# Attention in a two-layer decoder trunk: scaling and transposing the probabilities one unit further behind the exponentials

## The chip, the cores and the metric

The kernel runs on one core of one Trainium2 chip. The metric is the device time of one execution in microseconds (us). One execution was also profiled. A core has five engines that run their own instruction streams and wait for each other by semaphores: PE (TensorE, matrix products; its weight loads are shown apart as PEld), DVE (VectorE), ACT (ScalarE), POOL (GpSimd) and SP (SyncE, which here only issues DMAs).

## The reference

Two layers over 1024 tokens of width 1024, in fp32. Layer 0 projects the normalized input to six parts, runs a gated linear recurrence (mixer A) and a sliding-window attention (mixer B) on them, gates both and projects them back. Layer 1 is a gated MLP with spatial mixing over chunks of 128 tokens. The change lies in mixer B; what it computes for a block of 128 queries and 256 keys is this:

```python
sc = jnp.einsum("bqkgd,bskd->bkgqs", qblk, kblk).astype(jnp.float32) * scale + bias
sc = jnp.where(mask, sc, -jnp.inf)
m = jnp.maximum(jnp.max(sc, axis=-1, keepdims=True), sink)
p = jnp.exp(sc - m)
denom = jnp.sum(p, axis=-1, keepdims=True) + jnp.exp(sink - m)
out = jnp.einsum("bkgqs,bskd->bqkgd", (p / denom).astype(vblk.dtype), vblk)
```

Before it q and k are RMS-normalized; after it the result is multiplied by SiLU of its gate path. Mixer A is a causal convolution of width 4, two sigmoid gates by block-diagonal products, and a scan over the tokens:

```python
xa = causal_depthwise_conv(za, conv_w[j], conv_b[j])
ya = rg_lru(xa, gate_a_w[j], gate_a_b[j], gate_x_w[j], gate_x_b[j], lru_lambda[j])
```

## The kernel before

All large products are done as three fp32r products of split operands (high*high, high*low, low*high; `mm3`, lines 145 to 147), so a weight tile comes in two parts: ACT makes `wh` (line 133) and DVE makes `wl` (line 134) from the raw tile that SP fetched (line 125). `load_weights` does this some tiles ahead.

Attention is cut into 32 units: four groups c of four heads, times eight blocks b of 128 queries; unit u is c = u // 8, b = u % 8. A unit has these steps, each a helper:

- `att_bias(u)` writes the bias, times the RMS of q, into the tile `e` (four heads by 256 keys; 128 keys in block 0): two heads by one POOL instruction (line 524), two by ACT (line 521).
- `att_s(u)`: PE makes the scores in two PSUM banks `ps` (lines 545 and 546); DVE adds them to `e` and takes the row maxima (line 549, four times), then makes `es`, sink minus maximum (line 557).
- `att_exp(u)`: ACT takes the exponentials of `es` (line 563) and of `e` head by head with their sums (line 565).
- `att_scale(u)`: DVE adds the two halves of the keys (line 573, not in block 0), makes the denominator and its reciprocal (lines 575 and 576) and multiplies (line 577). Adding the halves is allowed because the value product below works with differences of neighbouring value blocks.
- `att_pt(u)`: PE transposes the four heads into the bank `ppt` (line 585), ACT copies it to `ph` (588), DVE makes the rest `pl` (589), and POOL masks both into `mh` and `ml` (595, not in block 0).
- `att_pv(u)`: PE multiplies by the values, two to four products (605); ACT copies halves to `ot` (609, 610).
- `att_out(u)`: DVE adds (616, 617) and POOL multiplies into the gated result `yb` (619).

The loop over t runs these steps for different units side by side, and between them fillers for PE: in each pass 12 products of a projection of q or of `za`, and 12 of one of the gate paths (`gb`, later `ga`); every second pass also squares and copies q (`q_parts`, lines 491 to 495) and sums the squares on PE (`st`, line 503). In passes where t % 8 is 2, 3, 4 or 6 a weight tile is split. After the units two more passes empty the pipeline, each with 24 products of `ga` of channel block 1. Then mixer A begins (`mix_a_conv`, `mix_a_split`, `mix_a_gates`, ...), with `za` of channel block 2 as the first products on PE: 48 of them.

In the loop the order on PE, ACT, DVE and POOL is the order of the code. The order of PE stays that of the code to the end, and that of ACT and DVE too up to the convolution of channel block 1, although instructions of steps that come later in the code may be put between; from there a scheduler orders ACT, DVE and POOL. SP is left to the scheduler in the loop and behind it. `e` and `ot` each have two buffers before.

Of the kernel before, what the change touches and what calls it, by code (L numbers as in the profile page):

```python
# [11 lines left out]
F32 = mybir.dt.float32  # L12
# [6 lines left out]
P = 128  # L19
S = 1024  # L20
D = 1024
NT = S // P
# [18 lines left out]
def bc(ap, pos, n):  # L41

    dims = [list(d) for d in ap.ap]
    dims.insert(pos, [0, n])
    return bass.AP(tensor=ap.tensor, offset=ap.offset, ap=dims)


def flip(ap):

    dims = [list(d) for d in ap.ap]  # L50
    step, n = dims[-1]
    dims[-1] = [-step, n]
    return bass.AP(tensor=ap.tensor, offset=ap.offset + step * (n - 1), ap=dims)
# [8 lines left out]
def trunk_kernel(  # L62
# [10 lines left out]
    const = ctx.enter_context(tc.tile_pool(name="const", bufs=1))  # L73
# [6 lines left out]
    def bank(name):  # L80
        return ps.tile([P, 512], F32, tag="p", name=name)
# [373 lines left out]
    at = p1.enter_context(tc.tile_pool(name="at", bufs=2, reuse_waits="tile"))  # L455
# [4 lines left out]
    def bias_tile(hp):  # L460
        if hp not in bias_tiles:
            bt = at.tile([P, 2, 256], F32, tag="bias", name=f"bias{hp}")
            src = bass.AP(tensor=rdram.tensor, offset=rdram.offset + hp * 2 * 384,
                          ap=[[1, P], [384, 2], [1, 256]])
            nc.sync.dma_start(out=bt, in_=src)
            bias_tiles[hp] = bt
        return bias_tiles[hp]
# [31 lines left out]
    def q_stats(hc, p, sq):  # L499

        acc = bank(f"st{hc}_{p}")
        for b in range(4):
            nc.tensor.matmul(acc[:, 2 * b:2 * b + 2], lhsT=sq[:, b, :], rhs=pair_ones, start=True, stop=True)
        m = small.tile([P, 8], F32, tag="qm", name=f"qm{hc}_{p}", bufs=2)
        rs = small.tile([P, 8], F32, tag="qrs", name=f"qrs{hc}_{p}", bufs=5)
        rms = small.tile([P, 8], F32, tag="qrms", name=f"qrms{hc}_{p}", bufs=5)
        nc.vector.tensor_scalar(out=m, in0=acc[:, :8], scalar1=1.0 / HD, scalar2=EPS, op0=ALU.mult, op1=ALU.add)
        nc.gpsimd.tensor_tensor(out=rs, in0=m, in1=half_neg, op=ALU.pow)
        nc.gpsimd.tensor_tensor(out=rms, in0=m, in1=rs, op=ALU.mult)
        q_state[hc][1].append((rs, rms))  # L510

    def att_bias(u):

        c, b = units[u]
        k0 = 0 if b else P
        e = at.tile([P, 4, 256], F32, tag="e", name=f"e{u}")
        for hp in range(2):
            rms = q_state[2 * c + b // 4][1][hp][1]
            if hp:
                for j in range(2):  # L520
                    nc.scalar.mul(e[:, 2 + j, k0:256], bias_tile(2 * c + hp)[:, j, k0:256],
                                  rms[:, 2 * (b % 4) + j:2 * (b % 4) + j + 1])
                continue
            nc.gpsimd.tensor_tensor(out=e[:, 2 * hp:2 * hp + 2, k0:256], in0=bias_tile(2 * c + hp)[:, :, k0:256],
                                    in1=bc(rms[:, 2 * (b % 4):2 * (b % 4) + 2], 2, 256 - k0), op=ALU.mult)
        state[u]["e"], state[u]["k0"] = e, k0
# [41 lines left out]
    def att_scale(u):  # L568
        st = state[u]
        e = st["e"]  # L570
        p = st["p"] = e[:, :, 0:P] if units[u][1] else e[:, :, P:256]
        if units[u][1]:
            nc.vector.tensor_tensor(out=p, in0=p, in1=e[:, :, P:256], op=ALU.add)
        den = small.tile([P, 4], F32, tag="den", name=f"den{u}")
        nc.vector.tensor_tensor(out=den, in0=st["sums"], in1=st["es"], op=ALU.add)
        nc.vector.reciprocal(out=den, in_=den)
        nc.vector.tensor_tensor(out=p, in0=p, in1=bc(den, 2, P), op=ALU.mult)
# [3 lines left out]
    def att_pt(u):  # L581
        st = state[u]
        pt = bank(f"ppt{u}")
        for h in range(4):
            nc.tensor.transpose(pt[:, h * P:(h + 1) * P], st["p"][:, h, :], ident)
        ptv = pt.rearrange("p (j i s) -> p i j s", j=2, i=2)
        ph, pl = [at.tile([P, 2, 2, P], F32R, tag=f"p{r}", name=f"p{r}{u}", bufs=1) for r in "hl"]
        nc.scalar.copy(out=ph, in_=ptv)
        nc.vector.tensor_tensor(out=pl, in0=ptv, in1=ph.bitcast(F32), op=ALU.subtract)
        st["parts"] = [part.rearrange("p i j s -> p (i j s)") for part in (ph, pl)]  # L590
        st["before"] = []
        if units[u][1]:
            for r, part in zip("hl", st["parts"]):
                m = at.tile([P, 512], F32R, tag=f"m{r}", name=f"m{r}{u}", bufs=1)
                nc.gpsimd.affine_select(out=m, in_=part.bitcast(F32), pattern=[[0, 4], [1, P]], compare_op=ALU.is_ge,
                                        fill=0.0, base=-P, channel_multiplier=1)
                st["before"].append(m)

    def att_pv(u):
        c, b = units[u]  # L600
        st = state[u]
        acc = bank(f"pv{u}")
        terms = [(v_all, part) for part in st["parts"]] + [(v_more, part) for part in st["before"]]
        for n, (v, part) in enumerate(terms):
            nc.tensor.matmul(acc, lhsT=v[:, b, c // 2].rearrange("p r d -> p (r d)"), rhs=part, start=n == 0,
                             stop=n == len(terms) - 1)

        ot = at.tile([P, 256], F32, tag="ot", name=f"ot{u}")
        nc.scalar.copy(out=ot[0:HD, :], in_=acc[HD:P, 0:256])
        nc.scalar.copy(out=ot[HD:P, :], in_=acc[0:HD, 256:512])  # L610
        st["acc"], st["ot"] = acc, ot

    def att_out(u):
        c, b = units[u]
        acc, ot = state[u]["acc"], state[u]["ot"]
        nc.vector.tensor_tensor(out=ot[0:HD, :], in0=acc[0:HD, 0:256], in1=ot[0:HD, :], op=ALU.add)
        nc.vector.tensor_tensor(out=ot[HD:P, :], in0=acc[HD:P, 256:512], in1=ot[HD:P, :], op=ALU.add)
        y = yb[c][:, :, b * P:(b + 1) * P]
        nc.gpsimd.tensor_tensor(out=y, in0=flip(ot.rearrange("p (j s) -> p j s", j=2)), in1=y, op=ALU.mult)
        state[u] = None  # L620
# [4 lines left out]
    def mix_a_part(n, kind, half, khalf):  # L625

        if khalf == 0:
            mix_acc[n, kind, half] = bank(f"{kind}{n}_{half}")
        proj_stationary_w(mix_acc[n, kind, half], (kind, n), hh, hl, half * 512, khalf * 4, khalf * 4 + 4)

    def mix_a_product(n, kind):
        for half in range(2):
            for kh in range(2):
                mix_a_part(n, kind, half, kh)
# [9 lines left out]
    NU = len(units)  # L644
# [7 lines left out]
        q_step(0, j)  # L652
    q_stats(0, 0, sq)
    sq = q_parts(0, 1)
    for t in range(NU + 2):
        c, b = divmod(t, NT)
        new = t < NU
        hc, j = t // 4 + 1, t % 4
        q_done, evac = False, None
        if t >= 2:  # L660
            att_pt(t - 2)
        if new:
            if hc < 8:
                q_done = q_step(hc, j)
            else:
                mix_a_part(1, "za", j // 2, j % 2)
            if t == 0:
                q_stats(0, 1, sq)
        if 1 <= t <= NU:
            att_exp(t - 1)  # L670
        if new:
            att_bias(t)
        if new and c and b == 0:
            gb_silu(c)
        if new:
            evac = gb_step(c + 1, b // 4, (b // 2) % 2, b % 2) if c < 3 else mix_a_first(b)
        else:
            for kh in range(2):
                mix_a_part(1, "ga", t - NU, kh)
        if 1 <= t <= NU:  # L680
            att_scale(t - 1)
        if new and b in SPLIT_STEPS:
            load_weights(SPLIT_STEPS[b] + 4 * c)
        sq = q_parts(hc, j // 2) if q_done else None
        if evac:
            nc.scalar.copy(out=evac[0], in_=evac[1])
        if t >= 2:
            att_pv(t - 2)
        if q_done:
            q_stats(hc, j // 2, sq)  # L690
        if new:
            att_s(t)
        if t >= 2:
            att_out(t - 2)
    manual.__exit__(None, None, None)
    p1.close()

    def load_x1(src, tiles):

# [224 lines left out]

    manual = tc.manual_schedule(engines={ET.Activation, ET.DVE})
    manual.__enter__()
    mix_a_product(2, "za")
    conv = mix_a_conv(0)
    split = mix_a_split(0, conv)
    ys = [mix_a_silu(0)]  # L930
# [37 lines left out]
    p4 = ExitStack()  # L968
    late = {"po": p4.enter_context(tc.tile_pool(name="po", bufs=1, reuse_waits="tile"))}
    h1h, h1l = [[None] * 2 for _ in range(2)], [[None] * 2 for _ in range(2)]  # L970
    st_all = const.tile([P, NT, 8, 6], F32, name="st_all")

    def v_stats(t, g, src):
        for i in range(2):
# [463 lines left out]
```

## Time and profile before

| | |
|---|---|
| median of 3 runs | 1363.16 us (1361.72 to 1363.23) |
| the profiled execution | 1363.54 us, its span 1361.8 us |
| granted TensorE clock, mean | 0.997 |
| PE busy | 1322.3 us (97% of the span) |
| DVE busy | 1005.3 us (74%) |
| ACT busy | 692.1 us (51%) |
| POOL busy | 208.4 us (15%) |

The span runs from the first to the last instruction. The units of attention run from 86 us to 381 us of it. Matmuls are pipelined and their recorded ends are modelled, so a matmul's recorded duration is longer than the distance to the next. A number in square brackets behind a row is the idle time of that engine just before the row, and what ended it.

### The profile page before, as it was taken

The page shows a single profiled execution, that of the slowest core. Times are in us where ns is not written, and L with a number is a line of the kernel's source. Part 1 is how long each engine was busy: PE and PEld are TensorE (multiplying, and loading weights), DVE is VectorE, ACT ScalarE, POOL GpSimd, SP SyncE. Part 2 cuts the span into 40 slices and gives each one's busy share as a digit, 9 for nine tenths or more (in the row PEclk, how much of TensorE's full clock was granted, in tenths as well). Part 3 has the DMA queues.
Part 4 walks back from the last instruction along what each step waited for, and adds up shares of the span by engine and source line. Part 5 has one row for each costly group of instructions (what it writes and reads, how often), then busy time and mean ns, then how long its engine had stood idle before and what let it go on. Part 6 is the DMA issues. An engine that isn't in the chain of part 4 may idle for free.

```text
span 1361.8 us, 17820 instructions
## 1 busy us (share of the span) xinstructions
PE 1322.3 (97%) x6775; PEld 1122.1 (82%) x6775; DVE 1005.3 (74%) x1622; ACT 692.1 (51%) x1246; POOL 208.4 (15%) x212
## 2 busy tenths in 40 slices
PE   7999999999999999999999999999999999999998
PEld 6987777777788788888888999888888888888887
DVE  6568888888868888996987656566657656679874
ACT  6466767676568778433553323244433444333431
POOL 3344444443313223000000000000000000000000
PEclk9999999999999999999999999999999999999999
DMA  6111111111211203521423232413332233496131
GB/s 222 32 48 48 32 47 32 47 32 48 63 43 39 65 9 124 216 78 74 141 87 101 93 117 86 155 54 101 118 116 76 95 109 108 160 376 251 47 109 62
DMA packets 97170, 131.38 MB, mean 96 GB/s; under 512 B 4907, under 2 KB 68540, under 8 KB 95036
## 3 DMA queue, kind: packets, MB, share of 16 engines
q1 hardware_dynamic: 97084, 130.24, 28.6%
q8 instruction: 53, 0.87, 0.3%
q14 instruction: 33, 0.27, 0.1%
HBM read 105.03 MB, written 25.19 MB: 96 GB/s over the span
## 4 chain that ended last, share of the span: by engine, by line
PE 67%; DVE 19%; ACT 7%; DMA 3%; issue 3%; SPq 0%; DVEq 0%; ACTq 0%
PE m L145 6%; PE m L147 6%; PE m L146 6%; PE u L145 4%; PE u L147 4%; PE u L146 4%; PE g L145 3%; PE g L146 3%; PE g L147 3%; ACT e L565 3%; PE v L145 3%; PE v L146 3%; PE v L147 3%; DVE e L549 3%; PE s L1319 2%
## 5 line engine op out<-in xcount | busy, mean ns | idle before, releaser
L145 PE MATMUL m<-wh_w,wa 128*128 128x512 f32 x432 | 168.6, 390 | 1.8 <-DVE x L844 1.8
L147 PE MATMUL m<-wh_w,wa 128*128 128x512 f32 x432 | 168.1, 389 | 0.0
L146 PE MATMUL m<-wl_w,wa 128*128 128x512 f32 x432 | 168.1, 389 | 0.0
L145 PEld LDWEIGHTS m<-wh_w,wa 128*128 128x128 f32 x432 | 81.1, 188 | 19.3 <-ACT wa L709 2.6
L147 PEld LDWEIGHTS m<-wh_w,wa 128*128 128x128 f32 x432 | 81.1, 188 | 16.9
L146 PEld LDWEIGHTS m<-wl_w,wa 128*128 128x128 f32 x432 | 81.1, 188 | 16.7
L716 ACT CAST wh_w<-b 128x1024 fp32r<-128x1024 f32 x36 | 37.7, 1048 | 74.5 <-DVE b L811 54.2
L134 DVE TENSOR_TENSOR wl<-raw,wh 128x1024 fp32r<-128x1024 f32 x38 | 51.6, 1362 | 19.0 <-ACT wh L133 18.9
L549 DVE CUSTOM_DVE_ANT_0 e<-ps,e,sink_bc 128x256 f32<-128x256 f32 (+1 forms) x128 | 62.3, 524 | 3.7 <-PE ps L546 3.2
L565 ACT ACTIVATE e<-e,nm 128x256 f32<-128x256 f32 (+1 forms) x128 | 61.4, 481 | 0.0
L844 DVE TENSOR_TENSOR x<-m,x 128x512 f32<-128x512 f32 x56 | 36.6, 686 | 29.4 <-PE m L147 29.4
L145 PE MATMUL ga<-hh,wh 128*128 128x512 f32 x128 | 50.8, 397 | 2.2 <-DVE ya L888 2.2
L145 PE MATMUL pq<-hh,wh 128*128 128x512 f32 x128 | 52.4, 410 | 0.0
L1291 ACT ACTIVATE sg<-sg 128x512 f32<-128x512 f32 x24 | 15.2, 632 | 70.9 <-DVE sg L1290 70.9
L147 PE MATMUL pq<-hh,wl 128*128 128x512 f32 x128 | 50.3, 393 | 0.0
L146 PE MATMUL ga<-hl,wh 128*128 128x512 f32 x128 | 50.3, 393 | 0.0
L145 PE MATMUL gb<-hh,wh 128*128 128x512 f32 x128 | 50.2, 392 | 0.0
L145 PE MATMUL za<-hh,wh 128*128 128x512 f32 x128 | 50.2, 392 | 0.0
L146 PE MATMUL pq<-hl,wh 128*128 128x512 f32 x128 | 50.1, 392 | 0.0
L147 PE MATMUL ga<-hh,wl 128*128 128x512 f32 x128 | 50.1, 391 | 0.0
L717 DVE TENSOR_TENSOR wl_w<-b,wh_w 128x1024 fp32r<-128x1024 f32 x36 | 46.3, 1285 | 5.0 <-ACT wh_w L716 4.8
L147 PE MATMUL gb<-hh,wl 128*128 128x512 f32 x128 | 49.9, 390 | 0.0
(401 smaller groups left out, 4040.0 us busy)
## 6 DMA issues: line engine op xcount, KB each, us to landing
raw<-in_w_in_a_dram SPq DMA_DIRECT2D x34, 512.0 KB, 4.0
b<-in_w_out_a_dram SPq DMA_DIRECT2D x22, 512.0 KB, 3.4
b<-in_w_out_c_dram SPq DMA_DIRECT2D x22, 512.0 KB, 6.0
rawg<-in_w_in_c_dram SPq DMA_DIRECT2D x16, 512.0 KB, 3.5
rawu<-in_w_in_c_dram SPq DMA_DIRECT2D x16, 512.0 KB, 3.4
vg<-vdram SPq DMA_DIRECT2D x8, 1024.0 KB, 6.9
ydram<-ug SPq DMA_DIRECT2D x32, 256.0 KB, 2.4
yg<-ydram SPq DMA_DIRECT2D x8, 1024.0 KB, 8.0
```

Of the source, the lines that this page charges most:

```text
L134: nc.vector.tensor_tensor(out=lo, in0=raws[j], in1=hi.bitcast(F32), op=ALU.subtract)
L145: nc.tensor.matmul(acc, lhsT=lh, rhs=rh, start=first, stop=False, skip_group_check=shared)
L146: nc.tensor.matmul(acc, lhsT=lh, rhs=rl, start=False, stop=False, skip_group_check=shared)
L147: nc.tensor.matmul(acc, lhsT=ll, rhs=rh, start=False, stop=last, skip_group_check=shared)
L549: nc.vector.tensor_tensor_reduce(out=e[:, h, k0:256], in0=acc[:, j * 256:j * 256 + kw], in1=e[:, h, k0:256], scale=rs[:, 2 * (b % 4) + j:2 ...
L565: nc.scalar.activation(out=e[:, h], in_=e[:, h], func=AF.Exp, bias=st["nm"][:, h:h + 1], accum_out=st["sums"][:, h:h + 1])
L716: nc.scalar.copy(out=hi, in_=src)
L717: nc.vector.tensor_tensor(out=lo, in0=src, in1=hi.bitcast(F32), op=ALU.subtract)
L844: nc.vector.tensor_tensor(out=dst, in0=accs[m], in1=dst, op=add)
L1291: nc.scalar.activation(out=c, in_=c, func=AF.Silu)
L1319: nc.tensor.matmul(acc[:, i * P:(i + 1) * P], lhsT=vgs[g][:, half * 4 + i, d * P:(d + 1) * P], rhs=ws_t[:, g, :], start=True, stop=True)
```

## The change

The loop has one pass more. `att_scale` moves from the middle of the pass, where it ran for unit t - 1 just after that unit's exponentials, to the start of the pass, where it runs for unit t - 2. `att_pt`, `att_pv` and `att_out` run for unit t - 3 where it was t - 2. `att_bias(t)` stands ahead of `att_exp(t - 1)`. `e` gets three buffers, `ot` one. The third emptying pass has 24 products of `za` of channel block 2 beside it, so only 24 of them stand behind the loop. The tile `st_all`, used in layer 1, moves to another pool.

```diff
-        e = at.tile([P, 4, 256], F32, tag="e", name=f"e{u}")
+        e = at.tile([P, 4, 256], F32, tag="e", name=f"e{u}", bufs=3)
...
-        ot = at.tile([P, 256], F32, tag="ot", name=f"ot{u}")
+        ot = at.tile([P, 256], F32, tag="ot", name=f"ot{u}", bufs=1)
...
-    for t in range(NU + 2):
+    for t in range(NU + 3):
...
-        if t >= 2:
-            att_pt(t - 2)
+        if 2 <= t < NU + 2:
+            att_scale(t - 2)
+        if t >= 3:
+            att_pt(t - 3)
...
+            att_bias(t)
         if 1 <= t <= NU:
             att_exp(t - 1)
-        if new:
-            att_bias(t)
...
-                mix_a_part(1, "ga", t - NU, kh)
-        if 1 <= t <= NU:
-            att_scale(t - 1)
+                mix_a_part(*((1, "ga", t - NU) if t < NU + 2 else (2, "za", 0)), kh)
...
-        if t >= 2:
-            att_pv(t - 2)
+        if t >= 3:
+            att_pv(t - 3)
...
-        if t >= 2:
-            att_out(t - 2)
+        if t >= 3:
+            att_out(t - 3)
...
-    mix_a_product(2, "za")
+    for kh in range(2):
+        mix_a_part(2, "za", 1, kh)
```

First place: DVE behind the output of unit 8 (`ot8`), to the first scores of the next unit. The digits behind a name are the unit, then a number of the tile. Before:

```order
L617 TENSOR_TENSOR ot8_1954<-pv8_1951,ot8_1954 64x256
L589 TENSOR_TENSOR pl9_1987<-ppt9_1981,ph9_1986 128x512
L573 TENSOR_TENSOR e10_1923<-e10_1923 128x4x128
L575 TENSOR_TENSOR den10_2028<-sums10_1959,es10_1976 128x4
L576 RECIPROCAL den10_2028<-den10_2028 128x4
L577 TENSOR_TENSOR e10_1923<-e10_1923,den10_2028 128x4x128
L134 TENSOR_TENSOR wl12_2033<-raw12_1569,wh12_2032 128x1024
L495 TENSOR_TENSOR qs3_1845<-pq3_1_1905,qs3_1845 64x512 x2
L507 TENSOR_SCALAR qm3_1_2058<-st3_1_2053 128x8
L549 ISA e11_2011,mx11_2064<-ps11_0_2067,e11_2011,sink_bc_97,qrs2_0_1483 128x256
```

And in the changed kernel, behind the same output:

```order
L617 TENSOR_TENSOR ot8_2021<-pv8_2018,ot8_2021 64x256
L573 TENSOR_TENSOR e10_1898<-e10_1898 128x4x128
L575 TENSOR_TENSOR den10_2060<-sums10_1936,es10_1953 128x4
L576 RECIPROCAL den10_2060<-den10_2060 128x4
L577 TENSOR_TENSOR e10_1898<-e10_1898,den10_2060 128x4x128
L589 TENSOR_TENSOR pl9_2070<-ppt9_2064,ph9_2069 128x512
L134 TENSOR_TENSOR wl13_2113<-raw13_1924,wh13_2112 128x1024
L549 ISA e12_2090,mx12_2126<-ps12_0_2129,e12_2090,sink_bc_97,qrs3_0_1839 128x256
```

The scaling of unit 10 now stands ahead of `pl` of unit 9, and what follows are the scores of unit 12, not 11.

Second place: ACT where attention ends and mixer A begins, from the output of unit 31. `xa0` and `xa1` are the convolutions of channel blocks 0 and 1, `gh0` a part of the gate weights, `r0` the first gate, made from the products `gt0` of PE. Before:

```order
L610 COPY ot31_4078<-pv31_4073 64x256
L866 ACTIVATE xa0_4165<-za0_3282,cols_96 128x1024
L897 CAST gh0_4228<-gr0_4225 128x256
L875 CAST xh0_4170<-xa0_4165 128x1024
L887 ACT_TABLE_LOAD
L887 ACTIVATE sg0_4174<-za0_3282 128x512 x2
L864 COPY z1_4180<-za1_0_3639 128x512
L864 COPY z1_4180<-za1_1_3814 128x512
L133 CAST wh27_4195<-raw27_4108 128x1024
L866 ACTIVATE xa1_4183<-z1_4180,cols_96 128x1024
```

And in the changed kernel:

```order
L610 COPY ot31_4103<-pv31_4098 64x256
L866 ACTIVATE xa0_4168<-za0_3258,cols_96 128x1024
L897 CAST gh0_4231<-gr0_4228 128x256
L133 CAST wh27_4198<-raw27_4136 128x1024
L875 CAST xh0_4173<-xa0_4168 128x1024
L887 ACT_TABLE_LOAD
L887 ACTIVATE sg0_4177<-za0_3258 128x512 x2
L864 COPY z1_4183<-za1_0_3615 128x512
L864 COPY z1_4183<-za1_1_3790 128x512
L906 ACTIVATE r0_4235<-gt0_0_0_4237,cols_96 128x512
L866 ACTIVATE xa1_4186<-z1_4183,cols_96 128x1024
```

The split of the weight tile 27 moved ahead of `xh0`, and the first gate ahead of the convolution of channel block 1.

## Rows read from the trace of the kernel before

**Rows 1.** Windows: stretch, us, busy us (instructions) of PE, PEld, DVE, ACT, POOL, PEclk.

```profile
247.00:319.00 72.00, 68.15 (x354) 56.29 (x353) 61.16 (x163) 50.45 (x135) 31.69 (x38) 1.00 0.14 38
319.00:372.00 53.00, 47.94 (x234) 39.20 (x232) 46.11 (x112) 32.63 (x92) 21.07 (x25) 0.97 0.24 69
```

**Rows 2.** Waits, 68 to 385 us: total us, times, longest us.

```profile
DVE e L573 <- ACT e L565: 21.7, 28, 1.6
...
PE ppt L585 <- DVE e L577: 11.7, 13, 1.2
```

**Rows 3.** Timeline of ACT, `es` of units 16 to 20, and 24: start us, us.

```profile
232.71 0.21 ACT L563 ACTIVATE es<-es 128x4 f32<-128x4 f32 x1
...
241.03 0.20 ACT L563 ACTIVATE es<-es 128x4 f32<-128x4 f32 x1 [2.02 <-DVE es L557]
...
248.76 0.21 ACT L563 ACTIVATE es<-es 128x4 f32<-128x4 f32 x1 [2.23 <-DVE es L557]
...
259.25 0.20 ACT L563 ACTIVATE es<-es 128x4 f32<-128x4 f32 x1 [2.82 <-DVE es L557]
...
267.99 0.21 ACT L563 ACTIVATE es<-es 128x4 f32<-128x4 f32 x1 [2.18 <-DVE es L557]
...
304.13 0.21 ACT L563 ACTIVATE es<-es 128x4 f32<-128x4 f32 x1
```

**Rows 4.** Timeline, one pass of the loop: DVE, POOL and PE.

```profile
203.35 0.54 DVE L549 CUSTOM_DVE_ANT_0 e<-ps,e,sink_bc 128x256 f32<-128x256 f32 x1
...
206.24 0.43 DVE L617 TENSOR_TENSOR ot<-pv,ot 64x256 f32<-64x256 f32 x1
...
206.69 0.69 DVE L589 TENSOR_TENSOR pl<-ppt,ph 128x512 fp32r<-128x512 f32 x1
206.74 0.73 POOL L619 TENSOR_TENSOR yb<-ot,yb 128x256 f32<-128x256 f32 x1 [1.42 <-DVE ot L617]
...
207.43 0.63 POOL L595 TENSOR_SCALAR_AFFINE_SELECT mh<-ph 128x512 fp32r<-128x512 f32 x1
...
208.02 0.63 POOL L595 TENSOR_SCALAR_AFFINE_SELECT ml<-pl 128x512 fp32r<-128x512 f32 x1
208.14 1.06 DVE L573 TENSOR_TENSOR e<-e 128x512 f32<-128x512 f32 x1 [0.75 <-ACT e L565]
...
208.62 1.47 POOL L524 TENSOR_TENSOR e<-bias,qrms 128x512 f32<-128x512 f32 x1
208.70 0.19 PEld L605 LDWEIGHTS pv<-ml,v_more 128*128 128x128 f32 x1 [0.33 <-POOL ml L595]
...
209.12 0.99 DVE L575 TENSOR_TENSOR den<-sums,es 128x4 f32<-128x4 f32 x1
...
210.36 0.69 DVE L577 TENSOR_TENSOR e<-e,den 128x512 f32<-128x512 f32 x1
210.97 1.22 DVE L134 TENSOR_TENSOR wl<-raw,wh 128x1024 fp32r<-128x1024 f32 x1
...
211.19 0.63 PE L585 MATMUL ppt<-ident,e 128*128 128x128 f32 x4 [1.05 <-DVE e L577]
```

**Rows 5.** Timeline, other passes: the sums of squares, q, and bias alone.

```profile
200.09 1.05 PE L503 MATMUL st<-pair_ones,sq 128*128 128x2 f32 x8
...
201.73 1.39 DVE L495 TENSOR_TENSOR qs<-pq,qs 64x512 fp32r<-64x512 f32 x2
...
360.53 1.03 POOL L524 TENSOR_TENSOR e<-bias,qrms 128x512 f32<-128x512 f32 x1
```

**Rows 6.** Timeline, end of attention and start of mixer A.

```profile
378.20 0.39 PE L605 MATMUL pv<-ml,v_more 128*128 128x512 f32 x1
...
384.71 0.43 DVE L898 TENSOR_TENSOR gl<-gr,gh 128x256 fp32r<-128x256 f32 x1 [2.27 <-ACT gh L897]
...
400.65 2.65 DVE L876 TENSOR_TENSOR xl<-xa,xh 128x1024 fp32r<-128x1024 f32 x1 [0.87 <-ACT xh L875]
...
402.95 0.39 PE L145 MATMUL gt<-xh,gh 128*128 128x512 f32 x1
```

More of the change, by code (lines that the diff above doesn't have):

```diff
@@ L692, in trunk_kernel @@
             att_s(t)
-        if t >= 2:
-            att_out(t - 2)
+        if t >= 3:
+            att_out(t - 3)
     manual.__exit__(None, None, None)
     p1.close()
+    const_c = ctx.enter_context(tc.tile_pool(name="const_c", bufs=1))
     def load_x1(src, tiles):
@@ L970, in trunk_kernel @@
     h1h, h1l = [[None] * 2 for _ in range(2)], [[None] * 2 for _ in range(2)]
-    st_all = const.tile([P, NT, 8, 6], F32, name="st_all")
+    st_all = const_c.tile([P, NT, 8, 6], F32, name="st_all")
     def v_stats(t, g, src):
```

## The prediction

> **What bounds the kernel now.** I read the windows first. In the loop of attention PE is busy 68.15 of 72 us, so 3.85 us in every eight units are idle; in the loop's last stretch 5.06 of 53 us are idle and the granted clock is 0.97 [rows 1]. PE is short of work there, but not by much. The list of waits says for whom: PE waits 11.7 us for the scaled probabilities before it can transpose them (13 times), and DVE waits 21.7 us for the exponentials (28 times) before it can scale [rows 2]. The `es` of units 16 and 24 stand 71.42 us apart, so eight units take that long [rows 3].
>
> One pass in the timeline shows the loop that sets this [rows 4]. I count from T, the end of the second output instruction (206.24 + 0.43 = 206.67). DVE's scores and outputs take 206.67 - 203.35 = 3.32 us up to T. Then `pl` runs to T + 0.7, DVE idles 0.75 us, the add of the halves takes 1.06, the denominator 0.99, and the multiplication ends at 211.05, T + 4.38. Only then can the next scores go. The add and the denominator are long because POOL works: the add starts at 208.14 while `ml` runs to 208.65, and ends 0.55 after that; the bias on POOL starts at 208.62 but ends 0.89 after the add, and takes 1.47 here against 1.03 in a pass where no such DVE operation holds it up [rows 4, 5]; the denominator, 128x4, ends with the bias. So DVE operations with two SBUF operands and POOL's take turns. `pl`, which reads PSUM, keeps its 0.69 beside POOL's `yb`.
>
> This loop gives 3.32 + 4.38 = 7.70 us for a plain pass. A pass with a weight split adds 1.13 (distance 210.97 to 212.10; its row is 1.22, overlapped by 0.09) and one with q 1.39 + 0.17. Measured between the `es` rows: 7.73 for unit 18 (split, but POOL has no masks to make for block 0, so the denominator meets nothing), 10.49 for unit 19 (split and q, sum 10.39), 8.74 for unit 20 (split, sum 8.83) [rows 3]. The loop over DVE and the exponentials explains every pass within 0.1 us, so it bounds the stage, not PE.
>
> **The change, part by part.** The wait for the exponentials goes: DVE scales unit t - 2, whose exponentials ended a pass ago. The wait of PE for the scaling goes with it. What is late next: `pl` now stands behind the scaling on DVE, POOL's `ml` behind `pl`, POOL's bias of the coming unit behind `ml`, and DVE's scores behind that bias. In the kernel before, `pl` came first and the bias was done long before the scores.
>
> The new pass from T, by the same rows. Add T + 0.02 to 0.71. POOL's `yb` (0.73) is asked for at 0.07, waits and ends at 1.3; the denominator ends with it, reciprocal 0.2 more, the multiplication could start at 1.57 but `mh` (0.63) holds POOL's side until 1.89, so it ends 0.55 later, at 2.44. `pl` follows to 3.05, `ml` to 3.74, the bias (1.03) to 4.73, scores from 4.8. A plain pass is then 3.32 + 4.8 = 8.12 us, longer than 7.70. With a split: `wl` goes before `ml` (4.19), then `ml` 4.74, bias 5.73, scores 5.8, so 9.1 against 8.74. With q: `qs` reads PSUM and lies beside `ml` and the bias, so it costs DVE nothing; here PE decides: `ml` at 3.74, then its value product, `st` (about 0.95 of its 1.05 [rows 5]) and the scores' first bank, 1.9 us together, 5.7: 9.05. Split and q with no masks (block 3): 9.35 against 10.49. Without the add (block 2) 8.0; behind the half-sized block 0, 8.7; block 0, with half a bias, 7.9. One each of 7.9, 8.7, 8.0 and 9.35, with 9.1 and 9.05 twice each, is 70.25 us for eight units, 1.2 less than now. Passes with q gain, passes with only a split lose. Over the 25 units in the steady state that is 3.8 us.
>
> In the first three passes DVE has less to do than now and PE is the bound; three passes without their 0.48 us of idle time (3.85/8) give 1.4. In the last stretch PE loses idle time and clock together, 5.06 us and 0.03 x 53 = 1.6 [rows 1]; of this I estimate 3.0 as saved, since its waits for the scaling are the largest kind [rows 2] and a late exponential now has a pass to spare. Together PE loses 8.2 us less by the end of attention. The third buffer of `e` and the one buffer of `ot` cost nothing in this: the bias of t waits for transposes of t - 3 at the start of the pass, long over, and `ot` is free when `yb` ends at T + 1.3, well before the next copy.
>
> **What is given back.** One pass more empties the pipeline, and its filler, 24 products, formerly stood behind the last value product. From 378.20 to 402.95 PE starts 109 matmuls (one value product, 48 + 24 + 24 fillers, 12 gates), 0.227 us each [rows 6], so 24 are 5.5 us. ACT and DVE begin mixer A only behind the output of unit 31. Before, the last value product is at 378.20, and the gates of channel block 1 wait on PE for `xl`, which ends at 403.30, against 402.95 when PE got there [rows 6]: no slack. With 24 products less in between PE comes 5.5 us too early. The same ACT and DVE work gets shorter by about 2.2: DVE's `gl` waited 2.27 for gate weights [rows 6], whose DMA sits in SP's queue behind a weight load that waits for a `wl` of the last pass; that `wl` is now one unit earlier. The split of tile 27 is only moved within that stretch, not added. So 5.5 - 2.2 = 3.3 come back as idle time of PE, and idle time of that length may bring the granted clock down for a while, as in the last stretch (0.97); I add 0.8, half of the 1.6 above. Scheduled reorderings behind that count as nothing, bounded by the idle time of PE in the rest of mixer A, about 2 us either way.
>
> Sum: -8.2 + 3.3 + 0.8 = -4.1 us on the profiled 1363.54: 1359.4. The median lies 0.4 lower, so I forecast 1359.0.
>
> Bounds of the terms no row shows as they will be: the pass lies between 67.6 us per eight units (71.42 less all 3.85 idle) and, with the collisions of the port falling the other way, about 73; the handover between 5.5 and 0.
>
> **Rivals.**
> *PE-bound.* If POOL's operations fit between DVE's without collisions, `pl` ends at T + 2.3, and PE loses no time. All of 17 us idle (3.85 in each 72 us over 225 us, and 5.06) and 1.6 of clock go; less 3.3 given back: -15, 1348. For it: DVE was busy only 61.16 of 72. Against it: four POOL operations and four two-operand DVE operations follow on the same T. Chance 0.13.
> *Given back.* The stage gains as I say but the handover takes it all, because the gate weights do not come earlier and PE waits the full 5.5 us; or the gain is half. The first gives -4.1 + 2.2 = -1.9, the second 0: 1361 to 1363. Chance 0.24.
> *Slower.* At T POOL takes the port first. Then `yb` runs to 0.8, the add to 1.35, `mh` to 1.9, the denominator and the multiplication to 2.75, `pl` to 3.4: each pass with masks is 0.35 longer than in my sum, 9 us over 26 passes, and the result is +5, 1368. It decides early: the forecast is used up if `pl` ends 0.15 us later than T + 3.05. For it: the request of POOL comes only 0.05 us behind DVE's at 206.74 against 206.69 [rows 4]. Against it: in the rows the operation that asked first went first. [...] Chance 0.18.
> *The forecast* has 0.45, with its own range of 1355 to 1361.
>
> **How the numbers follow.** About 0.2% (2.7 us) is what a measurement of this kernel can tell from no change. Faster by more: 0.13 from the PE-bound case, about 0.37 of the forecast's 0.45, and 0.08 of the given-back case, 0.58. Slower by more: 0.17 of the slower case and a little of the given-back one, 0.20. The rest, 0.22, is the same. The range goes from the PE-bound case to near the slower one: 1348 to 1367.
>
> **What would show it.** Right: no wait of the add for exponentials, no wait of `ppt` for the scaling; waits of PE for `ml` and of DVE's scores for the bias instead; the add at 0.69, but the multiplication lengthened by `mh`; eight units in about 70 us; PE idle near 3 us before the gates of channel block 1. Wrong: eight units over 71.4 us, `pl` ending later than T + 3.2, or no PE idle time left in the loop at all.

## The result and the profile after

The changed kernel takes 1376.97 us (median of 4 runs, 1374.56 to 1378.07), against 1363.2 us before (4 runs, 1361.72 to 1363.53). The ratio is 1.0101, with a 95% interval of 1.0083 to 1.0118: 13.8 us slower, where 4.1 us faster was forecast. The profiled execution took 1376.04 us, its span is 1374.3 us, 12.5 more than before, and its mean granted clock 0.994 against 0.997.

The waits that the change was to remove are gone: between 68 and 385 us neither the add of the halves nor `ppt` waits for anything [rows 2]. Waits after, same stretch (total us, times, longest us):

```profile
DVE e L549 <- PE ps L546: 28.8, 23, 3.2
...
PEld pv L605 <- DVE pl L589: 17.4, 21, 2.4
PEld pv L605 <- POOL ml L595: 16.3, 21, 1.3
...
PE pv L605 <- POOL ml L595: 8.0, 9, 0.9
PE pv L605 <- DVE pl L589: 7.5, 8, 1.9
...
DVE e L549 <- POOL e L524: 3.7, 4, 0.9
```

PE now waits 15.5 us (8.0 + 7.5) for the value product's operands `pl` and `ml`, and DVE's scores wait 28.8 us for the products `ps` that stand behind it on PE. The bias was named as the last step ahead of the scores; it is that in 4 passes only.

Windows after (columns as in [rows 1]): PE is busy 68.42 of 72 us where it was 68.15, and 46.72 of 53 where it was 47.94.

```profile
247.00:319.00 72.00, 68.42 (x352) 55.39 (x351) 59.81 (x160) 50.52 (x136) 36.21 (x38) 1.00 0.13 37
319.00:372.00 53.00, 46.72 (x223) 37.20 (x222) 45.05 (x112) 32.29 (x91) 24.51 (x22) 0.97 0.23 66
```

ACT's `es` rows after, units 16 to 24 (answers to [rows 3]):

```profile
232.33 0.20 ACT L563 ACTIVATE es<-es 128x4 f32<-128x4 f32 x1
...
240.14 0.20 ACT L563 ACTIVATE es<-es 128x4 f32<-128x4 f32 x1 [0.35 <-DVE es L557]
...
248.25 0.21 ACT L563 ACTIVATE es<-es 128x4 f32<-128x4 f32 x1 [0.64 <-DVE es L557]
...
258.19 0.19 ACT L563 ACTIVATE es<-es 128x4 f32<-128x4 f32 x1
...
267.24 0.20 ACT L563 ACTIVATE es<-es 128x4 f32<-128x4 f32 x1 [0.35 <-DVE es L557]
...
276.49 0.20 ACT L563 ACTIVATE es<-es 128x4 f32<-128x4 f32 x1 [0.35 <-DVE es L557]
...
285.78 0.21 ACT L563 ACTIVATE es<-es 128x4 f32<-128x4 f32 x1 [0.35 <-DVE es L557]
...
295.36 0.19 ACT L563 ACTIVATE es<-es 128x4 f32<-128x4 f32 x1
...
304.28 0.20 ACT L563 ACTIVATE es<-es 128x4 f32<-128x4 f32 x1
```

Eight units take 304.28 - 232.33 = 71.95 us; 71.42 before, 70.25 forecast.

One pass with q in the timeline after (start us, us; the bracket is idle time and what ended it). T is the end of L617, 195.59 + 0.43 = 196.02:

```profile
195.59 0.43 DVE L617 TENSOR_TENSOR ot<-pv,ot 64x256 f32<-64x256 f32 x1
...
196.04 0.69 DVE L573 TENSOR_TENSOR e<-e 128x512 f32<-128x512 f32 x1
...
196.09 1.24 POOL L619 TENSOR_TENSOR yb<-ot,yb 128x256 f32<-128x256 f32 x1 [3.57 <-DVE ot L617]
...
196.65 0.70 DVE L575 TENSOR_TENSOR den<-sums,es 128x4 f32<-128x4 f32 x1
...
197.29 0.62 POOL L595 TENSOR_SCALAR_AFFINE_SELECT mh<-ph 128x512 fp32r<-128x512 f32 x1
...
197.60 0.86 DVE L577 TENSOR_TENSOR e<-e,den 128x512 f32<-128x512 f32 x1
...
198.49 0.69 DVE L589 TENSOR_TENSOR pl<-ppt,ph 128x512 fp32r<-128x512 f32 x1
...
199.26 0.63 POOL L595 TENSOR_SCALAR_AFFINE_SELECT ml<-pl 128x512 fp32r<-128x512 f32 x1 [1.34 <-DVE pl L589]
...
199.94 0.50 PE L605 MATMUL pv<-ml,v_more 128*128 128x512 f32 x1
...
201.97 0.54 DVE L549 CUSTOM_DVE_ANT_0 e<-ps,e,sink_bc 128x256 f32<-128x256 f32 x1 [0.53 <-PE ps L546]
```

The collisions came as worked out: `yb` takes 1.24 us instead of 0.73, the denominator 0.70 for 128x4, `mh` holds up the multiplication, which ends at T + 2.44, as forecast. `pl` ends at T + 3.16 (3.05 forecast), `ml` at T + 3.87 (3.74), the scores start at T + 5.95 (5.7).

Where mixer A begins, PE waits five times, three times for ACT and twice for DVE's `xl`, 4.76 us together (0.94, 1.42, 1.35, 0.76 and, later, 0.29). Behind the fourth wait its matmuls stand 0.43 us apart instead of 0.23 for about 3 us, at a granted clock of 0.50 from 412.8 to 416.0; its mean is 0.94 between 400 and 430 us:

```profile
400.79 0.50 PE L145 MATMUL gt<-xh,gh 128*128 128x512 f32 x1 [0.94 <-ACT z L864]
...
404.55 0.50 PE L145 MATMUL ga<-hh,wh 128*128 128x512 f32 x1 [1.42 <-ACT r L906]
...
411.63 0.50 PE L145 MATMUL gt<-xh,gh 128*128 128x512 f32 x1 [1.35 <-ACT xh L875]
412.89 0.79 PE L146 MATMUL gt<-xl,gh 128*128 128x512 f32 x1 [0.76 <-DVE xl L876]
...
414.34 0.63 PE L146 MATMUL gt<-xl,gh 128*128 128x512 f32 x1
```

And in the output projection of mixer A, which the forecast counted as nothing, PE waits for `x`, whose addition stands behind a late weight tile; the wait was 1.37 us before:

```profile
590.37 0.77 PE L145 MATMUL m<-wh_w,wa 128*128 128x512 f32 x1 [3.67 <-DVE x L844]
590.94 0.63 PE L146 MATMUL m<-wl_w,wa 128*128 128x512 f32 x1
```

Behind this wait too the granted clock is lower: 0.50 from 590.3 to 593.5, where the rows stand 0.43 us apart, and 0.56 from 590.3 to 594.0. Before the change it was 1.00 behind the wait of 1.37 (579.4 to 583.0). So 2.3 us are lost by the longer wait and about 1.4 by the clock: seven matmuls take 3.13 us here (590.37 to 593.50) and 1.68 before (579.46 to 581.14).

The span's 12.5 us fall into three pieces. The last value product (`pv<-ml` of unit 31) is at 387.51, 9.31 later than at [rows 6]; 5.45 of that are the 24 fillers that now stand ahead of it (0.227 us each), so attention itself lost 3.9. The first `m<-wh_w,wa` matmul, in the output projection, is at 548.45 (539.83 before), 8.62 later: 4.8 lost in the handover (8.62 - 3.86; the fillers cancel out). The first `v<-whv,gh` matmul, in layer 1, is at 751.5 (739.1): 12.4 later, so 3.7 in the output projection. What follows lost 0.1.

### The profile page after: what moved, and what is told of

It is laid out like the page before. It is cut to its first block, busy times and chain, and to the rows that moved or that the text cites. A ratio compares the mean times of both kernels' runs of the same rounds, so it can differ in the third digit from the quotient of the medians.

```text
span 1374.3 us, 17785 instructions
## 1 busy us (share of the span) xinstructions
PE 1329.9 (97%) x6775; PEld 1123.6 (82%) x6775; DVE 1000.4 (73%) x1622; ACT 691.9 (50%) x1246; POOL 229.7 (17%) x212
## 4 chain that ended last, share of the span: by engine, by line
PE 68%; DVE 18%; ACT 4%; DMA 4%; issue 3%; POOL 2%; SPq 0%; DVEq 0%; ACTq 0%; POOLq 0%
PE m L145 6%; PE m L147 6%; PE m L146 6%; PE u L145 4%; PE u L146 4%; PE u L147 4%; PE g L145 3%; PE g L146 3%; PE g L147 3%; DVE e L549 3%; PE v L145 3%; PE v L147 3%; PE v L146 3%; PE s L1320 2%; PE pv L605 2%
## 5 line engine op out<-in xcount | busy, mean ns | idle before, releaser
L549 DVE CUSTOM_DVE_ANT_0 e<-ps,e,sink_bc 128x256 f32<-128x256 f32 (+1 forms) x128 | 62.4, 525 | 32.7 <-PE ps L546 28.8
L134 DVE TENSOR_TENSOR wl<-raw,wh 128x1024 fp32r<-128x1024 f32 x38 | 51.3, 1357 | 17.4 <-ACT wh L133 17.2
L619 POOL TENSOR_TENSOR yb<-ot,yb 128x256 f32<-128x256 f32 x32 | 37.1, 1159 | 90.1 <-DVE ot L617 90.1
```

The lines of the kernel that those rows point to most:

```text
L134: nc.vector.tensor_tensor(out=lo, in0=raws[j], in1=hi.bitcast(F32), op=ALU.subtract)
L549: nc.vector.tensor_tensor_reduce(out=e[:, h, k0:256], in0=acc[:, j * 256:j * 256 + kw], in1=e[:, h, k0:256], scale=rs[:, 2 * (b % 4) + j:2 ...
```

## The experiments

The kernel before was run beside each group of experiments (medians 1362.43, 1362.84 and 1363.48 us), and ratios are to that. Three theories stood at the start. A: the pass through `pl`, `ml` and the value product sets the loop, because the scaling now stands ahead of `pl`. B: the emptying passes' fillers cost the handover. C: the buffers and the moved pool cost time by themselves.

**`pl` first.** The transposes of t - 3 stand ahead of the scaling of t - 2; on DVE only `pl` changes place.

```diff
-        if 2 <= t < NU + 2:
-            att_scale(t - 2)
         if t >= 3:
             att_pt(t - 3)
+        if 2 <= t < NU + 2:
+            att_scale(t - 2)
```

> The changed kernel with two calls swapped: transposes of unit t - 3 (and so pl) ahead of the scaling of unit t - 2; only DVE's order differs. Theory A (scaling, pl, ml, value product in a row set the pass): pl ends at T + 0.7 again instead of T + 3.16, ml near T + 2.6, PE no longer waits for ml, eight units fall from 71.95 to about 67.5 us, the time by 14 to 15, to 1362; what the handover and the output projection cost stays. Theory B (the loss is the handover to mixer A) and C (the loss is from the tiles' places in memory): eight units stay at 72, the time at 1377.

Measured: 1348.61 us (1347.38 to 1348.96), ratio to before 0.9895 (0.988 to 0.991): 28.4 us less than the changed kernel, where A expected 14 to 15. By position in the trace 23.3 of it lie ahead of the last value product (364.17). Another 3.7 lie in the output projection, which the edit does not touch: PE's wait for `x` is 1.5 us here, for a reason that the last experiment shows. One pass with q, T = 188.08:

```profile
188.11 0.69 DVE L589 TENSOR_TENSOR pl<-ppt,ph 128x512 fp32r<-128x512 f32 x1
188.15 0.74 POOL L619 TENSOR_TENSOR yb<-ot,yb 128x256 f32<-128x256 f32 x1 [4.38 <-DVE ot L617]
...
188.71 0.72 DVE L573 TENSOR_TENSOR e<-e 128x512 f32<-128x512 f32 x1
...
188.84 1.09 POOL L595 TENSOR_SCALAR_AFFINE_SELECT mh<-ph 128x512 fp32r<-128x512 f32 x1
...
189.89 0.63 POOL L595 TENSOR_SCALAR_AFFINE_SELECT ml<-pl 128x512 fp32r<-128x512 f32 x1
...
192.72 0.54 DVE L549 CUSTOM_DVE_ANT_0 e<-ps,e,sink_bc 128x256 f32<-128x256 f32 x1
```

`pl`, which reads PSUM, takes 0.69 us beside `yb`, as it does with POOL idle (0.69, without `yb`, below), and `yb` takes 0.74 beside it, where it took 1.24 beside the add. `ml` ends at T + 2.44 instead of T + 3.87, the scores start at T + 4.64 instead of T + 5.95, and no bracket stands behind them. Eight units take 66.29 us (287.27 - 220.98), and the window shows PE with hardly a gap:

```profile
220.98 0.20 ACT L563 ACTIVATE es<-es 128x4 f32<-128x4 f32 x1
...
287.27 0.21 ACT L563 ACTIVATE es<-es 128x4 f32<-128x4 f32 x1
```

```profile
247.00:319.00 72.00, 71.72 (x381) 60.53 (x380) 66.12 (x171) 54.56 (x145) 38.60 (x42) 1.00 0.13 38
```

So the loop here is bound by PE. A holds, with its size underestimated, and for a reason that the window itself shows: before, PE had 354 matmuls in 72 us [rows 1], here 381. A matmul that waits for its operand is recorded longer here (`pv<-ml` has a median of 0.50 us in the changed kernel, as in the pass above, and of 0.40 before the change), so busy time hid part of PE's slack: before the change 3.85 us were idle per 72 us by the window, but 5.13 us are gained per eight units (71.42 - 66.29).

**Fillers respread.** 24 + 12 + 12 products of `ga` in the three emptying passes, all 48 of `za` behind them, as before.

```diff
-            for kh in range(2):
-                mix_a_part(*((1, "ga", t - NU) if t < NU + 2 else (2, "za", 0)), kh)
+            for half, kh in (((0, 0), (0, 1)), ((1, 0),), ((1, 1),))[t - NU]:
+                mix_a_part(1, "ga", half, kh)
...
-    for kh in range(2):
-        mix_a_part(2, "za", 1, kh)
+    mix_a_product(2, "za")
```

> The changed kernel with only its fillers of the emptying passes spread anew: 24, 12 and 12 products of ga, and all 48 of za of channel block 2 behind the loop, as before. Theory B: the 4.8 us that PE lost between the last value product and the gates of channel block 1 come back less up to 2 us of new waits in the two thin passes: 1372 to 1374. Theory A alone: the same 1377, passes of the loop unchanged at 71.95 us per eight units.

Measured: 1372.76 us (1369.34 to 1374.85), ratio 1.007 (1.0049 to 1.0092): 4.2 less than the changed kernel. The loop stayed (71.83 us per eight units), and the waits before the gates went: in the stretch where PE was busy 25.39 of 30 us at a clock of 0.94, the row is now

```profile
400.00:430.00 30.00, 29.99 (x131) 24.24 (x130) 24.57 (x21) 26.50 (x32) 8.05 (x3) 1.00 0.16 45
```

From the last value product to the first `m<-wh_w,wa` it is 161.7 us (384.0 to 545.7), as before the change (161.6). The 4.8 us of the handover are back, so B holds. But 24 fillers fewer (5.45 us) bring the last value product only 3.5 us forward: the two thinner passes cost 2.0 in new waits, and 2.7 are left at the first `m<-wh_w,wa`.

**Memory only.** The kernel before, with three buffers for `e`, one for `ot`, and `st_all` in its own pool; the order is that of before.

```diff
-        e = at.tile([P, 4, 256], F32, tag="e", name=f"e{u}")
+        e = at.tile([P, 4, 256], F32, tag="e", name=f"e{u}", bufs=3)
-        ot = at.tile([P, 256], F32, tag="ot", name=f"ot{u}")
+        ot = at.tile([P, 256], F32, tag="ot", name=f"ot{u}", bufs=1)
...
-    st_all = const.tile([P, NT, 8, 6], F32, name="st_all")
+    st_all = const_c.tile([P, NT, 8, 6], F32, name="st_all")
```

> The kernel before with only the buffers (three of e, one of ot) and the pool of st_all changed; the order on every engine is that of the kernel before. Theories A and B: 1363, no difference. Theory C: the output projection of layer 0 loses 3.7 us as in the changed kernel, 1367.

Measured: 1363.51 us (1361.38 to 1364.18), ratio 1.0002 (0.9993 to 1.0012). C falls.

**Both.** `pl` first and the fillers respread, the two diffs above together.

> Both edits, pl ahead of the scaling and the fillers spread anew. Theories A and B together: 1377 - 15 - 4 = 1358, faster than the kernel before by about 5 us. If the two losses are one and the same wait, no better than the first of them alone, 1362.

Measured: 1345.05 us (1343.36 to 1346.18), ratio 0.9869 (0.9855 to 0.9884): faster than both kernels, by 17.4 us than before. The two effects add up (28.4 and 3.6; 23.3 and 4.1 at the last value product, where the second has 24 fillers fewer ahead of it). `za` behind the loop and `pl` ahead of the scaling is the form in which this change pays.

**Without `yb`.** The changed kernel without POOL's multiplication of line 619; the output is not gated.

```diff
-        nc.gpsimd.tensor_tensor(out=y, in0=flip(ot.rearrange("p (j s) -> p j s", j=2)), in1=y, op=ALU.mult)
```

> The changed kernel without POOL's multiplication into yb (it leaves out the gating of the attention output; its DVE, PE and ACT work is as in the changed kernel). Theory A, sharpened: in the changed kernel the pass is set by the chain from T over the port collisions to pl, ml, the value products and the next scores. Without yb the denominator needs not wait for POOL and pl ends near T + 2.8 instead of T + 3.16: about 0.36 us less in each of 28 masked units, eight units in 69.5 us instead of 71.95, 1367 in all. Rival: the chain is set by PE's own work and the collision with yb is covered: eight units stay at 71.9 us, 1376 to 1377.

Measured: 1360.59 us (1355.59 to 1365.54), ratio to before 0.9985 (0.9971 to 0.9999), 16.4 less than the changed kernel; 9 to 10 was expected. One pass, T = 199.69 + 0.43 = 200.12:

```profile
200.15 0.69 DVE L573 TENSOR_TENSOR e<-e 128x512 f32<-128x512 f32 x1
...
200.75 0.15 DVE L575 TENSOR_TENSOR den<-sums,es 128x4 f32<-128x4 f32 x1
...
200.94 0.18 DVE L576 RECIPROCAL den<-den 128x4 f32<-128x4 f32 x1
...
201.16 0.69 DVE L577 TENSOR_TENSOR e<-e,den 128x512 f32<-128x512 f32 x1
...
201.88 0.69 DVE L589 TENSOR_TENSOR pl<-ppt,ph 128x512 fp32r<-128x512 f32 x1
```

Without POOL beside it the denominator takes 0.15 us, not 0.70, the multiplication 0.69, not 0.86, and `pl` ends at T + 2.45 instead of T + 3.16. Eight units take 68.78 us (225.97 to 294.75), 3.17 less, 0.45 per unit with masks. That is 12 us of the 16. The rest is not traced: the profiled execution is the slowest of the ten and only 10.5 us below that of the changed kernel, and the times go with the mean granted clock of the single executions (0.992 in this one and in the next slowest, 1364.92 us; 0.994 to 0.998 in the other eight, 1355.59 to 1361.64).

**`pl` first, without `yb`.** The same line left out of the kernel with `pl` first.

> The kernel with pl ahead of the scaling (measured 1348.6), also without POOL's multiplication into yb. Theory A: with pl first the collisions lie beside PE's work, which fills 71.8 of 72 us, so the same deletion is worth nothing: 1347.5 to 1349.5, eight units in 66.3 us. Rival: the port collisions still set the pass there and the gain of pl first is only a shorter chain: eight units fall by 1 us or more, 1344 or less.

Measured: 1345.88 us (1344.24 to 1347.34), ratio 0.9876 (0.9862 to 0.9891): 2.7 less than with `yb`, against 16.4 in the changed kernel. Eight units 65.91 us (220.14 to 286.05) instead of 66.29. The time lies midway between the two expectations, the loop nearer the first (0.4 us per eight units, where the rival wanted 1 or more): the same collisions are nearly covered once `pl` is out of their way.

**Scaling put back.** The kernel with both, but the scaling for unit t - 1 at its old place; only transposes, values and output are one unit later than before.

```diff
-        if 2 <= t < NU + 2:
-            att_scale(t - 2)
...
+        if 1 <= t <= NU:
+            att_scale(t - 1)
         if new and b in SPLIT_STEPS:
...
```

> The kernel with pl first and the respread emptying passes (measured 1345.05), with the scaling put back to its old place: for unit t - 1, behind that unit's exponentials; transposes, values and output stay one unit later than before. What the prediction said of the kernel before, that the loop over DVE and the exponentials bounds the stage: DVE waits about 20 us for exponentials again, eight units take 71 to 71.5 us, 1362 to 1364. Rival: what bounded it was PE's wait for the scaled probabilities (11.7 us), which stays away here: eight units in 67 to 68.5 us, 1347 to 1353.

Measured: 1362.82 us (1361.36 to 1365.09, 10 runs), ratio 1.0003 (0.9994 to 1.0013). Eight units take 70.78 us (230.40 to 301.18), and DVE's wait is back:

```profile
230.40 0.21 ACT L563 ACTIVATE es<-es 128x4 f32<-128x4 f32 x1
...
301.18 0.20 ACT L563 ACTIVATE es<-es 128x4 f32<-128x4 f32 x1
```

```profile
DVE e L573 <- ACT e L565: 24.4, 28, 2.2
```

PE's wait for the scaled probabilities is gone here and gained 0.6 us per eight units; moving the scaling as well gains 4.3 more (66.49). That the loop over DVE and the exponentials bounded the stage before is thereby shown. That the whole is no faster than before lies in the output projection: the last value product is 4.1 us earlier than before, the first `v<-whv,gh` 0.7 later, and PE waits 4.6 us for `x` in between (the last experiment).

**The changed kernel again**, for a second profile of the output projection.

> The changed kernel once more, for a second profile. PE's wait for x in the output projection of mixer A was 3.7 us here and 4.6 us in the kernel with respread emptying passes, against 1.4 to 1.6 us in all the others. If the late weight tile belongs to the kernel, 3.5 us or more again; if it belongs to single executions, 1.4 to 1.6 us, and a time some 2 us lower.

Measured: 1375.03 us (one run), PE's wait for `x` 3.5 us, ACT's for the tile `b` 10.2 (10.4 in the first profile, 8.1 before): the tile is late in both profiles, so it belongs to the kernel. In the handover PE's waits are 5.9 us here and the granted clock stays at 1.00 from 400 to 430 us, where the first profile had 4.8 us and 0.94; the stretch from the last value product to the first `m<-wh_w,wa` is as long (160.9 us in both).

**Instruction packet moved.** In the DMA view of the changed kernel (a window of 16 us in 40 slices, centred on the first of that group of loads; share in tenths, GB/s, and the packets of the instruction queue):

```profile
DMA  0459960000000000000100358997887597999999
GB/s 0 97 179 399 394 241 0 0 0 0 0 0 0 0 0 0 0 0 0 41 0 0 77 102 317 394 312 256 246 241 256 179 225 287 394 369 369 430 379 420
...
q8 instruction: 1, 0.02, 0.4%
```

The lone 41 in the 20th slice is a packet on the instruction queue q8, just ahead of the loads (their first is issued in the middle of the window), and from the 28th slice on the rate is 179 to 287 GB/s for seven slices, 2.8 us, where it is about 400 later. In the five profiles with the late tile the packet lies within half a microsecond of that first load; in the five without it 1.6 to 4.0 us ahead. Such packets come every 27 to 36 us between 400 and 600 us in the profiles before and after, where PE is busy nearly throughout (196.4 and 191.7 of 200 us), so they may be PE's own instructions. Then 20 transposes that nothing reads, on PE in its first 9 idle us, should move the packet:

```diff
+    pad = bank("pad")
+    for j in range(20):
+        nc.tensor.transpose(pad[:, (j % 4) * P:(j % 4 + 1) * P], ident, ident)
```

> The changed kernel with 20 more transposes of the identity on PE at its start, where PE idles 9 us; nothing reads them. They move every later fetch of PE's instructions (one packet on q8 about every 28 us) earlier by 40 instructions, about 4 us at some 9 instructions per us. In the five profiles where DMA b comes late (wait of 10.2 to 11.3 us) such a packet lies within 0.5 us of the first of that group of loads; in the five where it comes in time (8.1) it lies 2 to 4 us ahead. If the fetch is the cause: wait for DMA b 8.1 us, PE's wait for x 1.4 to 1.6 instead of 3.7 us, and 2 to 2.5 us less, 1374 to 1375. If it only goes along: 10 us, 3.5 us and 1376 to 1377.5 again.

> The same 20 transposes in the kernel with the scaling put back to its old place (measured 1362.8, PE's wait for x 4.6 us). If the fetch is the cause: wait for DMA b 8.1 us instead of 11.3, PE's wait for x 1.4 to 1.6, 3 us less, 1359.3 to 1360.5. If it only goes along: 1362 to 1364.

Measured in the changed kernel: 1371.38 us (1370.21 to 1373.59), ratio to before 1.0051 (1.0034 to 1.0068). The packet is now 4.4 us ahead. It moved by some 4 us, about what 20 weight loads and 20 matmuls of PE take (0.227 us for one of each [rows 6], 4.5 us), which speaks for PE as its owner. The dip is shorter, the wait for `b` 8.1 us (10.4), PE's for `x` 1.5 (3.67):

```profile
DMA  0659930010000000000000267967999999999999
GB/s 15 148 220 394 389 144 0 0 41 0 0 0 0 0 0 0 0 0 0 0 0 0 92 205 236 312 174 241 379 404 384 446 425 379 451 410 420 430 389 451
```

From the first `m<-wh_w,wa` to the first `v<-whv,gh` it is 199.34 us (549.77 to 749.11), as before the change (199.31), and 203.05 in the changed kernel. The profiled executions differ by only 2.45 (1373.59 and 1376.04), because this one lost 1.6 ahead of the first `m<-wh_w,wa`, with a mean granted clock of 0.99 from 430 to 540 us (481 matmuls), where the changed kernel had 1.00 (486). The medians differ by 5.6 us, more than the 2 to 2.5 expected; what goes beyond 3.7 I have not traced. In the kernel with the scaling put back: 1359.76 us (1357.87 to 1361.46), ratio 0.9972 (0.9961 to 0.9984), 3.1 less, as expected, with waits of 8.5 (11.3) and 1.8 us (4.6); the same stretch takes 201.4 us instead of 203.9, so here 2 us stay. No run has a shift of PE's stream that leaves the packet beside the loads, so a rival by which any shift would do is not tested. What went with the packet was 2 to 3 us of later loads: waits for `b` of 10.2 to 11.3 us with it beside them, 8.1 to 8.5 without.

## Why the prediction was wrong

Term by term, by positions in the profiled executions: the steady state, forecast at -3.8, came out at +3.3 us, the last stretch at +3.7 instead of -3.0, the first passes at -3.2 instead of -1.4. So attention, forecast at -8.2, lost 3.8. The handover came out at +4.8 (+4.1), the output projection at +3.7 (0). That is 12.4 us instead of -4.1 up to the first `v<-whv,gh`.

- **What bounded the loop before: right.** The waits for exponentials and scaling were the bound, and both go; the experiment with the scaling put back gives 70.78 us per eight units, all else as in the best version with 66.49. (The prediction's sums reach five of the eight passes; for the three around block 0 it gave none.)
- **The collisions of DVE and POOL: right in order and size.** Add, `yb`, denominator, `mh` and multiplication came in the order forecast, T + 2.44 to the hundredth. POOL did not go first: the add, 0.05 us ahead of `yb` (196.04 and 196.09), kept 0.69 and `yb` took 1.24, so what the slower rival supposed did not happen. What the prediction and the expectations call the port stands in no row; the rows show that operations of the two engines take longer beside each other (0.70 instead of 0.15 for the denominator).
- **"Scores 4.8" and the sum of 70.25 us: this step failed.** Distances of `es` rows against the forecast: block 3 (split and q, no masks) 9.94 against 9.35; the two passes with q 9.25 and 9.58 against 9.05; the two with a split 9.05 and 9.29 against 9.1; block 2 8.11 against 8.0; blocks 0 and 1 together 16.73 against 16.6. Together 1.7 us. I had counted `pl` as 0.61, the distance of two rows that overlap, instead of 0.03 + 0.69, and 1.9 us from the end of `ml` to the scores, where the pass shown has 2.08. In block 3 the bias, with no masks ahead of it, met the multiplication (1.28 us), and `pl`, `wl` and `qs` then stood one behind another. Small errors, in a sum whose whole gain was 1.2: eight units lost 0.5 us instead, where the steady state was to gain. Units 3 to 24 lost 3.3 together, 2.2 of it up to unit 8, right behind the shortened first passes. What these passes wait for is PE's value product and the scores behind it (23 waits for `ps`), and the bias, which the sum had last in every pass with a split and no q, in 4 passes only.
- **The last stretch, -3.0: this step failed too, wrong in sign.** From the `es` of unit 24 to that of unit 31 it takes 1.5 us longer than before, and the emptying 2.2 longer. The forecast took the idle time there to go with the waits for the scaling. They went (3.0 us), but from 312 to 388 us PE now waits 6.1 us for `pl` and `ml` (1.1 before, 312 to 380): the same chain sets these passes too. The clock there, counted as part of the gain, stayed at 0.97.
- **The first passes, -1.4: right in sign.** Up to the `es` of unit 3 they were 3.2 us shorter, more than forecast; what lies behind them took it back.
- **The handover, +4.1: right in size, 4.8 by position, in part by luck.** The two experiments give 4.2 and 3.6 in all, net of new waits in the thinner passes. `gl` no longer waits 2.27 us for gate weights, as forecast, but the 2.2 us did not come: `xl` of channel block 1 ends 25.3 us behind the last value product (412.84 - 387.51), 25.1 before (403.30 - 378.20). In place of that wait the split of tile 27, which the forecast took as only moved, stands ahead of `xh0` and itself waits 2.9 us for PE. So PE idles 4.8 us (5.9 in the second profile) instead of 3.3, partly ahead of the place named (for `z` and `r`), and against this stand 2.2 us of waits for `ya` that it had before in this stretch and has no longer, which the forecast did not count.
- **Reorderings behind it, counted as nothing within 2: wrong.** The output projection lost 3.7 us, 2.3 by a longer wait and 1.4 by the clock behind it, with an instruction packet beside a group of loads where before it came 3.6 to 4.0 us ahead; the 20 transposes, which moved the packet, took the 3.7 us away in this kernel and 2.6 of 4.6 in the one with the scaling put back.
- The lower bound of the pass, 67.6 us (71.42 less all idle time), was no bound: 66.29 was reached. And what I missed beside the sum was the order within DVE's part of the pass. The text named `pl` as "what is late next" and then priced it, without asking what the change would give with `pl` ahead of the scaling: there the chip does what the PE-bound rival, given 0.13 and 1348, describes (1348.61), though not by its condition: the collisions remain (the multiplication of that pass takes 0.87 us), but PE no longer waits behind them.

## What to carry to other kernels

When a step is taken off one chain by moving it to the start of a pass, look at what it now stands ahead of: work that another engine waits for goes first, work whose result is wanted a pass later goes behind it. Where a forecast gain per pass (here 0.15 us of 8.8) is smaller than the error of a chain of six rows, give the sign of that term no more than an even chance. Fillers that keep PE busy over a handover belong where the other engines need time, not where there happens to be one more pass. And before an edit gets the whole difference of two times, compare positions in the traces: 3.7 of the 28.4 us lay in a stage that the edit does not touch.

## What the hardware showed that I had not expected

- An instruction packet within 0.5 us of a group of DMA loads went with nearly 3 us of 180 to 290 GB/s instead of about 400, and the tile wanted from that group came 2 to 3 us later; with the packet 4.4 us ahead the waits were 8.1 and 8.5 us, near the 8.1 of the other profiles without it. Why one packet slows the loads for so long stays open.
- A denominator of 128x4 took 0.15 us with POOL idle and 0.70 beside `yb`; POOL's `yb` took 0.73 beside `pl` and 1.24 beside the add, its mask `mh` 0.63 [rows 4] or, beside the add and the denominator, 1.09. `pl`, with one operand in PSUM, took 0.68 to 0.69 in all 32 units, before and after.
- Behind PE's wait of 3.67 us the granted clock was 0.56 for 3.7 us (0.50 for the first 3.2), which cost some 1.4 us on top of the longer wait.
